# One inference step of a decoder layer on one core: residual pieces fetched ahead, the sample rows' norm in three parts, an earlier token norm, another order of six matmuls

## The chip, the cores and the metric

The kernel runs on one NeuronCore of a Trainium2 chip. The core has five engines with a queue of their own each: TensorE (PE in the profile, with its weight loads as PEld), VectorE (DVE), ScalarE (ACT), GpSimd (POOL) and SyncE (SP), which here issues the DMA transfers. The metric is the device time of one execution in microseconds. For a kernel the median of several runs is given.

## The reference

One layer of a hybrid decoder is computed for 1024 prompt tokens and for 8 samples of 4 new tokens (32 rows), with the same weights. All numbers are 32 bit.

```python
u, v, cq, ckv, kpe = split_in(rms_norm(x, g_mix) @ w_in)
a_out = chunk_gmlp(u, v, w_s, b_s, ln_g, ln_b)              # gated mixing in chunks of 128, width 512
q = mla_queries(rms_norm(cq, g_q_a) @ w_uq)                 # 8 heads, 64 + 32 rope, QK norm
k, vv = mla_keys_values(rms_norm(ckv, g_kv_a), kpe)         # samples: 4096 cached keys beside the new ones
b_out = causal_attention(q, k, vv)                          # width 512
x = x + concat(rms_norm(a_out), rms_norm(b_out)) @ w_o      # output projection, 1024 x 1024
x = x + mem_attend(rms_norm(x, g_mem_x), mk, mv)            # 4 heads x 128, 256 memory tokens
x = x + conv_ffn(rms_norm(x, g_ffn))                        # width 2816, causal convolution of 3
```

The caches, the memory keys and values and the convolution's last rows are results too.

## The kernel before, in words

A 32-bit operand of a matmul is kept as a high and a low part (`split`, lines 200 to 207): ACT casts the source to the high part, DVE subtracts it from the source, which gives the low part. `mm3` (line 185) makes a product from three matmuls per block of the inner dimension: high by high, high by low and low by high.

The stages follow each other: `phase1` (input projection), `phase2a` (attention of the prompt, from about 180 to 400 us), `phase2b` (attention of the samples over the cached pages), `mem_kv` (memory keys and values), `out_proj`, `mem_attention` and the feed-forward part. Inside a block `manual_schedule` the order of the named engines' instructions is the order in which the code issues them. Engines that are not named, and the interleaving of neighbouring blocks, are left to a planner.

**Attention of the prompt.** Units of one head and one half of the queries are cut into steps, 46 in all and a few more. A step transposes probabilities (L1038), computes scores (L1019) of a coming unit, whose maxima DVE takes (L1021, L1025), and multiplies by the values (L1053). Everything else is hung on steps by number with `put(list, steps)`: the splits of the second half's weights, the preparation of keys and queries of a head (`head_prep`, L988 with split L200 to L207), and the projection groups with their norms. `tok_s` is the group of the 32 sample rows for the first four heads: an allocation, two projections, and seven calls that advance a generator, `norm`. Its five parts that do something are: three products on 32 x 4 numbers (L943 to L945); the start of an inverse root (L250 to L252); its first and its second iteration (L259 to L264, four DVE instructions each); and the scaling of the queries with a copy (L954, L955, L959), followed by four POOL instructions for the rotary part (L637 to L640). The rotated queries are wanted when the sample stage starts at step 32.

**Output projection.** The 1056 tokens are three chunks c of 384, 384 and 288 columns (the last 32 are the sample rows), and the 1024 outputs are eight blocks m of 128. `chunk(m, c)` loads the residual piece (L1832, one of four `res` buffers), issues 24 matmuls and returns a function that adds the residual on DVE (L1837), stores the sum (L1838), splits it and squares it on ACT (L1908, L1911). The mixed rows, operands of the matmuls, come from DRAM in eight loads (L1792, three `raw` buffers) and are split in eight calls `split()`: four for chunk 1, then four for chunk 2. `tail[1]`, `tail[2]` and `end()` finish the last sample's attention (L1560 and L1572, then L1333); `mem_out()` issues the six stores of the memory keys and values (L1728, L1730). `mixed_sample` norms the sample rows: square with sum (L1812), inverse root on DVE (L250 to L264), scaling (L1814), then on PE four transposes (L1818), then four splits into chunk 2's operands. SP, PE, ACT and DVE follow the written order in this block.

**Memory attention.** 16 pairs of a head and 256 tokens pass through `scores`, softmax, `trans` (transposition, then a split into `th` and `tl`) and `values`, which multiplies them by the memory values `vh`, `vl` and writes PSUM bank `t`.

Of the kernel before, what the change touches and what calls it, by code (L numbers as in the profile page):

```python
# [5 lines left out]
F32 = mybir.dt.float32  # L6
# [7 lines left out]
P = 128  # L14
# [7 lines left out]
CH = [(0, 384), (384, 384), (768, 288)]  # L22
# [131 lines left out]
class Net:  # L154
# [41 lines left out]
    def split(self, hi, lo, src, g=None, eng="act"):  # L196

        nc, first = self.nc, None
        if g is None:
            first = {"act": nc.scalar.copy, "pool": nc.gpsimd.tensor_copy, "dve": nc.vector.tensor_copy}[eng](hi, src)  # L200
            low = lambda: nc.vector.tensor_tensor(lo, src, hi, ALU.subtract)  # L201
        else:
            if eng == "act":
                first = nc.scalar.activation(hi, src, AF.Copy, scale=g)
            else:
                {"pool": nc.gpsimd, "dve": nc.vector}[eng].tensor_scalar(hi, src, g, None, ALU.mult)
            low = lambda: nc.vector.scalar_tensor_tensor(lo, src, g, hi, ALU.mult, ALU.subtract)  # L207
        if self.lows is None:
            self.low = low()
        else:  # L210
            self.lows.append(low)
        return first
# [463 lines left out]
    def phase2a(self):  # L676
        nc, tc, I, O = self.nc, self.tc, self.I, self.O
        p = self.open("p2q")
# [4 lines left out]
        p = self.open("p2")  # L683
# [19 lines left out]
        c = {"ggq": ggq, "cmask": cmask, "rq": rq, "kss": self.kss, "qt": self.qt}  # L703
# [24 lines left out]
        tok_s, _ = self.proj_group(p, pp, 0, *groups[2], st[0], c)  # L728
# [12 lines left out]
        def put(fs, ts):  # L741
            for f, t in zip(fs, ts):
                extra[t].append(f)
# [5 lines left out]
                jobs[starts[n - 1] + at[e]].append((units[n], e))  # L749

        put(split_w, (7, 8, 13, 15))
        put(tok_s, (4, 4, 5, 17, 18, 19, 20, 21, 21, 21))
        put(preps[1][2:], (3, 4))
        for h in range(2, 8):
            b = 7 * (h - 1)
# [27 lines left out]

        E = mybir.EngineType
        with tc.manual_schedule(engines={E.PE, E.Activation, E.DVE, E.Pool}):
            for f in preps[0][0], preps[0][1], v1[0], norm[0], norm[1]:
# [399 lines left out]
    def phase2b(self):  # L1186
# [22 lines left out]
        def at(n, pos, f, *a):  # L1209
            ev.setdefault((n, pos), []).append(lambda: f(*a))  # L1210
# [38 lines left out]
        for b in range(NB):  # L1249
# [17 lines left out]
            for k, pos, f in ((0, 3, tail[0]), (2, 2, tail[1]), (3 if b == NB - 2 else 4, 3, tail[2])):  # L1267
                if b < NB - 1:
                    at(n + k, pos, f)
        E = mybir.EngineType  # L1270

# [43 lines left out]

        with tc.manual_schedule(engines={E.PE, E.Activation, E.DVE, E.Pool}):
            steps(-10, last + 1)

        with tc.manual_schedule(engines={E.SP, E.PE, E.Activation, E.DVE}):
            self.close("ps3")  # L1320
# [486 lines left out]
    def mixed_sample(self, p, pp, hi, lo):  # L1807

        nc = self.nc
        n = self.t(p, [NS, 512], F32, "n")  # L1810
        r = self.t(p, [NS, 1], F32, "r")
        nc.scalar.activation(n, self.b_s, AF.Square, accum_out=r)  # L1812
        self.rsqrt(p, r, r, 1.0 / 512)
        nc.scalar.activation(n, self.b_s, AF.Copy, scale=r)  # L1814
        yield
        tp = self.t(self.ppt, [P, 512], F32, "o", 1).rearrange("p (k n) -> p k n", k=4)[:, :, :NS]
        for k in range(4):
            nc.tensor.transpose(tp[:, k], n[:, k * P : k * P + P], self.ident[:NS, :NS])  # L1818
        for k in range(4):
            self.split(hi[:, k], lo[:, k], tp[:, k], self.col("g_ab", 4 + k))  # L1820
        yield

    def out_proj(self, pp, p, mxs, load, split, tail, xh, xl, r3, end):
        nc, I = self.nc, self.I
        acc, ws = self.acc, self.ws
        self.pad(acc[2], 2)

        def chunk(m, c):
            o, n = CH[c]
            wh, wl = ws[m]  # L1830
            res = self.t(p, [P, 384], F32, "res", 4)[:, :n]
            nc.sync.dma_start(res, I["xT"][:, 8 * o + m * n : 8 * o + m * n + n])  # L1832
            ps = self.t(pp, [P, 512], F32, "b", 6)[:, :n]
            self.mm3(ps, [(wh[:, k], wl[:, k]) for k in range(8)], [(mxs[c][0][:, k], mxs[c][1][:, k]) for k in range(8)])

            def out():
                nc.vector.tensor_tensor(res, ps, res, ALU.add)  # L1837
                nc.sync.dma_start(self.res_dram[:, m, o : o + n], res)  # L1838
                w = min(NP_ - o, n)
                self.split(xh[:, m, NS + o : NS + o + w], xl[:, m, NS + o : NS + o + w], res[:, :w])  # L1840
                if c == 2:
                    self.split(xh[:, m, :NS], xl[:, m, :NS], res[:, w:])
                self.square(self.pm, acc[c][:, :n], res, m)

            return out

        sample = self.mixed_sample(p, pp, *(x[:, 4:, 256:] for x in mxs[2]))
        E = mybir.EngineType
        with self.tc.manual_schedule(engines={E.SP, E.PE, E.Activation, E.DVE}):
            for _ in range(3):  # L1850
                load()
            split()
            load()
            x = chunk(0, 0)
            split()
            load()
            tail[1]()
            split()
            load()
            self.mem_out()  # L1860
            x()
            split()
            load()
            x = chunk(1, 0)
            tail[2]()
            x()
            split()
            load()
            x = chunk(2, 0)
            end()  # L1870
            split()
            w3 = self.t(self.wr, [P, 8, P], F32, "raw")
            nc.sync.dma_start(w3, I["w_o"][3])
            x()
            x = chunk(0, 1)
            split()
            split()
            next(sample)
            x()
            x = chunk(1, 1)  # L1880
            next(sample)
            x()
            chunk(2, 1)()
            chunk(0, 2)()
            ws[3] = self.stream(None, 8, raw=w3)
            chunk(1, 2)()
            chunk(2, 2)()
        for m in range(3, 10):
            if m > 4:
                chunk(m - 2, 2)()  # L1890
            if m < 7:
                ws[m + 1] = self.stream(I["w_o"][m + 1], 8)
            if m < 8:
                chunk(m, 0)()
                chunk(m, 1)()
        for c in range(2):
            self.token_roots(p, self.t(self.ppt, [P, 512], F32, "om"[c], 1), r3, c)
# [17 lines left out]
    def mem_attention(self, xh, xl, r3):  # L1915
        nc, tc, I, O = self.nc, self.tc, self.I, self.O
# [7 lines left out]
        ps_, p = self.open("pas"), self.open("pa")  # L1924
# [3 lines left out]
        vh, vl = (self.t(p, [P, 2, 512], FR, n) for n in ("vh", "vl"))  # L1928
# [20 lines left out]
        first = (0, 2, 5, 7)  # L1949
# [57 lines left out]
        def values(i):  # L2007
            h, g = units[i][0], order[units[i][1]]
            th, tl = ts.pop(i)
            t, hd = slice(g * 256, g * 256 + 256), slice(h * P, h * P + P)  # L2010
            ps = bank("t", 2)[:, :256]
            self.mm3(ps, [(vh[:, k, hd], vl[:, k, hd]) for k in range(2)], [(th[:, k], tl[:, k]) for k in range(2)])
            self.split(qh[:, h, t], ql[:, h, t], ps)


        sample = {}
# [76 lines left out]
        def slot(s):  # L2093
            c, h = divmod(s, 4)
            if s >= 5:
                scores(s - 5)
            if c > 1 and h == 0:
                roots(c - 1)
            query(h, c)
            if c == 1 and h == 0:  # L2100
                roots(0)
            if s >= 7:
                values(s - 7)
            if h == 3:
                square_sums(c)
            if s >= 6:
                trans(s - 6)
# [5 lines left out]
        with tc.manual_schedule(engines={E.PE}):  # L2113
# [26 lines left out]
            r = self.t(self.pw, [P, 10], F32, "hr")  # L2140
# [38 lines left out]
            for s in range(16, 23):  # L2179
                if s < 21:  # L2180
                    scores(s - 5)
                if s == 16:
                    roots(3)
                if s in VALUES:
                    sample_values(2 * VALUES.index(s))
                if s == 21:
                    sample_out()
                if s > 18:
                    ahead(*divmod(s - 19, 2))
                values(s - 7)  # L2190
                if s < 22:
                    trans(s - 6)
# [57 lines left out]
        for j in (1, 2, 3, 0):  # L2250
# [3 lines left out]
            if j == 2:  # L2254
                sums(0, q[:, 0])
                first = self.weights(0, NK, sums=0)
# [453 lines left out]
```

## Time and profile before

| what | value |
|---|---|
| median of 3 runs | 1813.22 us (1810.88 to 1813.76) |
| the profiled execution | 1813.55 us, its span 1811.8 us |
| mean granted clock of TensorE | 0.997 |
| PE busy | 1787.5 us, 99% of the span |
| DVE, ACT, POOL busy | 1349.3, 920.3, 697.4 us |
| moved by DMA | 261.05 MB, mean 144 GB/s |

A line of the profile names the line of the kernel, the engine, the operation, and result and operands as out<-in. "[2.67 <-DMA res<-xT]" behind an instruction says that its engine sat idle for 2.67 us before it and that the landing of the transfer `res<-xT` ended this. Lines of waits read: who waited, for whom, total in us, number of times, longest. Rows of stretches give, from a start to an end in us, the length, then for PE, PEld, DVE, ACT and POOL the busy time and the number of instructions, then TensorE's granted clock as a share of full speed, the share of DMA time and GB/s. Matmuls are pipelined, and their durations overlap in the timeline; the distance of two starts is what one costs.

### The profile page before, as it was taken

What the parts mean: (1) busy time and instruction counts of PE and PEld (TensorE: products, weight loads), DVE (VectorE), ACT (ScalarE), POOL (GpSimd) and SP (SyncE); (2) the same over time, 40 slices, a digit from 0 to 9 for tenths busy, and PEclk for the clock granted to TensorE, in tenths of its full rate; (3) what the DMA queues carried; (4) which work ended last, traced back from release to release, by engine and by line L of the source; (5) the groups of instructions that cost most, each with busy time, mean ns of one, the idle gap of its engine ahead of it and who ended that gap; (6) DMA issues with size and microseconds to landing.
All of it is one profiled execution on the core that took longest, in us unless ns stands there. A gap on an engine that the chain in (4) does not pass through costs nothing.

```text
span 1811.8 us, 39356 instructions
## 1 busy us (share of the span) xinstructions
PE 1787.5 (99%) x14254; PEld 1694.4 (94%) x14254; DVE 1349.3 (74%) x2777; ACT 920.3 (51%) x1930; POOL 697.4 (38%) x844
## 2 busy tenths in 40 slices
PE   9999999999999999999999999999999999999999
PEld 8999776769899999999799989999999999999999
DVE  7864767657688777787744678998888888878664
ACT  7335776766556555566434467433333333344442
POOL 1021656634445445552023001476677777400000
PEclk9999999999999999999999999999999999999999
DMA  8101353558776666664655245122222222585242
GB/s 324 48 18 62 118 188 117 181 167 227 213 212 179 197 190 190 173 193 127 185 167 189 103 161 184 63 92 86 72 71 81 73 78 88 154 314 165 88 147 78
DMA packets 153043, 261.05 MB, mean 144 GB/s; under 512 B 20881, under 2 KB 97394, under 8 KB 152850
## 3 DMA queue, kind: packets, MB, share of 16 engines
q1 hardware_dynamic: 152850, 258.55, 45.8%
q8 instruction: 112, 1.84, 0.4%
q14 instruction: 81, 0.66, 0.1%
HBM read 212.66 MB, written 45.82 MB: 143 GB/s over the span
## 4 chain that ended last, share of the span: by engine, by line
PE 75%; DVE 5%; ACT 3%; DMA 2%; issue 2%; SPq 1%; POOL 0%; DVEq 0%; ACTq 0%; POOLq 0%
PE s L185 19%; PE d L185 12%; PE E L185 7%; PE F L185 7%; PE X L185 7%; PE b L185 7%; PE A L185 3%; PE s L1019 2%; PE o L1053 2%; PE o L1548 2%; PE tp L1038 1%; PE tp L185 1%; DMA cT<-cT 1%; PE s L1426 1%; PE tp L988 1%
## 5 line engine op out<-in xcount | busy, mean ns | idle before, releaser
L185 PE MATMUL s<-w2h,ch 128*128 128x256 f32 x1018 | 302.6, 297 | 0.0
L185 PE MATMUL s<-w2h,cl 128*128 128x256 f32 x1018 | 294.4, 289 | 2.0 <-DVE cl L1411 2.0
L185 PE MATMUL s<-w2l,ch 128*128 128x256 f32 x1018 | 293.7, 289 | 0.0
L185 PEld LDWEIGHTS s<-w2h,ch 128*128 128x128 f32 x1018 | 192.3, 189 | 3.2 <-issue 2.9
L185 PEld LDWEIGHTS s<-w2h,cl 128*128 128x128 f32 x1018 | 192.1, 189 | 2.6 <-DVE cl L1411 2.2
L185 PEld LDWEIGHTS s<-w2l,ch 128*128 128x128 f32 x1018 | 192.5, 189 | 0.0
L1462 DVE TENSOR_REDUCE ss<-sq 128x16 f32<-128x1024 f32 x128 | 155.2, 1213 | 29.4 <-ACT sq L1459 29.3
L1411 POOL TENSOR_TENSOR cl<-cT,ch 128x512 fp32r<-128x512 f32 x64 | 86.2, 1346 | 195.3 <-ACT ch L1407 189.4
L1459 ACT ACTIVATE sq<-s 128x512 f32<-128x512 f32 x128 | 76.4, 597 | 72.9 <-PE s L185 72.7
L200 ACT CAST a<-brb 128x528 fp32r<-128x528 f32 x77 | 48.8, 634 | 109.4 <-PE d L185 108.2
L1456 ACT ACTIVATE sq<-s 128x512 f32<-128x512 f32 x128 | 76.6, 598 | 49.5 <-PE s L185 39.3
L201 DVE TENSOR_TENSOR a<-brb,a 128x528 fp32r<-128x528 f32 x77 | 54.1, 706 | 55.3 <-ACT a L200 55.1
L185 PE MATMUL d<-a,w 128*128 128x264 f32 x768 | 95.2, 285 | 0.0
L185 PEld LDWEIGHTS d<-a,w 128*128 128x128 f32 x768 | 94.2, 189 | 0.0
L2342 POOL TENSOR_TENSOR lo<-s,hi 128x1024 fp32r<-128x1024 f32 x20 | 63.8, 3190 | 45.7 <-ACT hi L2341 45.7
L2398 ACT COPY a<-A 128x264 f32<-128x264 f32 x43 | 16.1, 374 | 121.2 <-PE A L185 113.8
L185 PE MATMUL mm<-wlo,xh 128*128 128x256 f32 (+3 forms) x272 | 77.1, 286 | 0.1
L185 PE MATMUL mm<-whi,xh 128*128 128x256 f32 (+3 forms) x272 | 77.1, 285 | 0.0
L185 PE MATMUL mm<-whi,xl 128*128 128x256 f32 (+3 forms) x272 | 76.9, 287 | 0.0
L1407 ACT CAST ch<-cT 128x512 fp32r<-128x512 f32 x128 | 73.6, 628 | 0.2 <-issue 0.2
L2464 POOL TENSOR_TENSOR cv<-cv,row 128x1056 f32<-128x1056 f32 x22 | 65.1, 2960 | 20.4 <-ACT cv L2463 20.4
L185 PE MATMUL d<-a,hi 128*128 128x264 f32 x552 | 72.0, 285 | 0.0
(828 smaller groups left out, 6356.8 us busy)
## 6 DMA issues: line engine op xcount, KB each, us to landing
cT<-cT SPq DMA_DIRECT2D x256, 160.0 KB, 2.7
ck<-ck SPq DMA_DIRECT2D x256, 144.0 KB, 3.6
raw<-w_up SPq DMA_DIRECT2D x44, 512.0 KB, 3.6
wsumd<-wsum SPq DMA_DIRECT2D x26, 512.0 KB, 3.8
actd<-cv SPq DMA_DIRECT2D x44, 264.0 KB, 2.4
brb<-actd SPq DMA_DIRECT2D x44, 264.0 KB, 5.6
wsum<-w_down SPq DMA_DIRECT2D x22, 512.0 KB, 3.7
raw<-wsumd SPq DMA_DIRECT2D x20, 512.0 KB, 3.7
```

The costliest lines, as they stand in the source:

```text
L185: x = self.nc.tensor.matmul(out, l, r, start=first and i == 0, stop=last and i == len(seq) - 1)
L200: first = {"act": nc.scalar.copy, "pool": nc.gpsimd.tensor_copy, "dve": nc.vector.tensor_copy}[eng](hi, src)
L201: low = lambda: nc.vector.tensor_tensor(lo, src, hi, ALU.subtract)
L1019: nc.tensor.matmul(sv, a[:, tq], b[:, kc], start=i == 0, stop=i == 2)
L1053: nc.tensor.matmul(u["o"][g : g + 64, o : o + m * P], s["v"][:, j, h % 4], th[:, z * P : (z + m) * P], start=j == 0, stop=b == len(banks) - 1,
L1407: nc.scalar.copy(d["h"][:, k], src[k])
L1411: (nc.vector if k else nc.gpsimd).tensor_tensor(d["l"][:, k], src[k], d["h"][:, k], ALU.subtract)
L1456: nc.scalar.activation(sq[:, 0], ps[:, :, n0 : n0 + 256], AF.Square)
L1459: nc.scalar.activation(sq[:, 1], pt.rearrange("p (e d) -> p e d", e=2), AF.Square)
L1462: yield lambda: nc.vector.tensor_reduce(s["ss"][:, g0 : g0 + 2].rearrange("p e (z h) -> p z e h", z=2), sq.rearrange("p z e (h d) -> p z e ...
L2342: eng.tensor_tensor(lo, src, hi, ALU.subtract)
L2464: nc.gpsimd.tensor_tensor(cv, cv, row, ALU.mult)
```

## The change

- Sample rows of the first four heads: the five parts of `norm` move from steps 17, 18, 19, 20 and 21 to steps 10, 10, 12, 13 and 13.
- `mixed_sample` stops once more, between the inverse root and the scaling. In the output projection its three parts now stand before the sixth split, between the sixth and the seventh split, and before the eighth.
- Residual pieces: the first four are fetched behind the third load of mixed rows, each further one behind the residual step that frees a buffer; chunks past the ninth fetch for themselves as before.
- The first residual step and the matmuls of chunk (1, 0) stand ahead of `mem_out()` and the fourth split; the load of the fourth block's weights (`w3`) stands behind the seventh split instead of the sixth; the eighth split stands behind the sample's transposes.
- `values` in the memory attention: both blocks' two products with the high part `th` first, then the two with `tl`. The six matmuls are the same.

```diff
-        put(tok_s, (4, 4, 5, 17, 18, 19, 20, 21, 21, 21))
+        put(tok_s, (4, 4, 5, 10, 10, 12, 13, 13, 13, 13))
@@ mixed_sample
         self.rsqrt(p, r, r, 1.0 / 512)
+        yield
         nc.scalar.activation(n, self.b_s, AF.Copy, scale=r)
@@ out_proj
+        ready = []
+
+        def fetch(m, c):
+            o, n = CH[c]
+            res = self.t(p, [P, 384], F32, "res", 4)[:, :n]
+            nc.sync.dma_start(res, I["xT"][:, 8 * o + m * n : 8 * o + m * n + n])
+            ready.append(res)
+
         def chunk(m, c):
...
-            res = self.t(p, [P, 384], F32, "res", 4)[:, :n]
-            nc.sync.dma_start(res, I["xT"][:, 8 * o + m * n : 8 * o + m * n + n])
+            if not ready:
+                fetch(m, c)
+            res = ready.pop(0)
...
+        first = [(m, c) for c in range(3) for m in range(3)]
...
             for _ in range(3):
                 load()
+            for x in first[:4]:
+                fetch(*x)
             split()
             load()
             x = chunk(0, 0)
...
             split()
             load()
+            x()
+            x = chunk(1, 0)
             self.mem_out()
-            x()
             split()
             load()
-            x = chunk(1, 0)
             tail[2]()
             x()
+            fetch(*first[4])
+            x = chunk(2, 0)
+            end()
             split()
             load()
-            x = chunk(2, 0)
-            end()
+            x()
+            fetch(*first[5])
+            next(sample)
+            x = chunk(0, 1)
+            split()
+            next(sample)
             split()
             w3 = self.t(self.wr, [P, 8, P], F32, "raw")
             nc.sync.dma_start(w3, I["w_o"][3])
             x()
-            x = chunk(0, 1)
-            split()
-            split()
-            next(sample)
-            x()
+            fetch(*first[6])
             x = chunk(1, 1)
             next(sample)
+            split()
             x()
-            chunk(2, 1)()
+            fetch(*first[7])
+            x = chunk(2, 1)
+            x()
+            fetch(*first[8])
             chunk(0, 2)()
@@ values in mem_attention
-            self.mm3(ps, [(vh[:, k, hd], vl[:, k, hd]) for k in range(2)], [(th[:, k], tl[:, k]) for k in range(2)])
+            pairs = [(v[:, k, hd], th[:, k]) for k in range(2) for v in (vh, vl)] + [(vh[:, k, hd], tl[:, k]) for k in range(2)]
+            for n, (l, r) in enumerate(pairs):
+                nc.tensor.matmul(ps, l, r, start=n == 0, stop=n == 5)
```

## The prediction

> **What bounds the kernel now.** I read four views in this order: the busy times of the page, TensorE's (PE's) waits over the whole span, the timelines around the longest ones, and stretches of the timeline with their granted clock. First the page:
>
> ```profile
> PE 1787.5 (99%) x14254; PEld 1694.4 (94%) x14254; DVE 1349.3 (74%) x2777; ACT 920.3 (51%) x1930; POOL 697.4 (38%) x844
> ```
>
> PE is busy 1787.5 of 1811.8 us, so everything that a reordering can win lies in the remaining 24 us and in matmuls that run at a lower clock. The waits of PE, longest in total first:
>
> ```profile
> PE o L1818 <- ACT n L1814: 4.1, 1, 4.1
> PE tp L1038 <- ACT pr L1030: 3.0, 5, 1.1
> PE s L185 <- DVE cl L1411: 2.0, 1, 2.0
> PE s L1019 <- DVE pr L1025: 1.9, 5, 1.3
> PE tp L1066 <- DVE rsum L1061: 1.8, 2, 1.5
> PE st L361 <- DVE warm L356: 1.6, 1, 1.6
> PE tp L1038 <- DVE qTl L207: 1.5, 2, 1.3
> PE t L185 <- DVE tl L201: 1.4, 3, 0.7
> ```
>
> The columns are total, number, longest. The change touches the first (transposes of the sample rows in the output projection), the last (memory attention), and, as shown below, the longest single wait of the fourth, fifth and seventh. Around the first wait, stretches give PE, PEld, DVE, ACT and POOL busy time, then the granted clock:
>
> ```profile
> 898.52:902.72 4.20, 4.20 (x25) 4.04 (x24) 1.70 (x3) 1.95 (x5) 0.87 (x1) 1.00 0.83 263
> 902.72:907.02 4.30, 0.16 (x1) 0.00 (x0) 3.63 (x16) 1.88 (x6) 0.15 (x1) 0.74 0.66 205
> 907.02:907.58 0.56, 0.56 (x4) 0.50 (x4) 0.17 (x1) 0.56 (x2) 0.00 (x0) 0.50 0.94 386
> 907.58:911.58 4.00, 4.00 (x13) 4.00 (x13) 2.31 (x7) 2.20 (x7) 0.00 (x0) 0.50 0.38 130
> 911.58:913.72 2.14, 2.14 (x13) 2.14 (x13) 0.16 (x1) 0.00 (x0) 1.01 (x1) 0.98 0.55 167
> ```
>
> The stall is 4.30 us long and then goes on costing: the transposes and the first half of the next chunk run at a granted clock of 0.50. That half takes 4.00 us, the second half of the same chunk 2.14.
>
> **Output projection: why the rows are late, and what the change does.** SyncE's (SP's) queue, DVE and ACT before the stall, and the PE group that makes the sample's rows:
>
> ```profile
> 896.67 0.37 SPq L1792 DMA_DIRECT2D raw<-mix  x1
> 897.10 0.46 SPq L1832 DMA_DIRECT2D res<-xT  x1
> ...
> 901.14 0.42 SPq L1832 DMA_DIRECT2D res<-xT  x1
> ```
> ```profile
> 892.33 1.97 PE L1333 MATMUL m<-wuv,olT 128*32 128x64 f32 x32
> ```
> ```profile
> 900.17 0.56 DVE L1837 TENSOR_TENSOR res<-b,res 128x384 f32<-128x384 f32 x1 [2.67 <-DMA res<-xT]
> ...
> 904.26 0.13 DVE L250 TENSOR_SCALAR rqx<-r 32x1 f32<-32x1 f32 x1
> ...
> 906.05 0.15 DVE L264 SCALAR_TENSOR_TENSOR r<-rqh,rqy 32x1 f32<-32x1 f32 x1
> ```
> ```profile
> 901.61 1.69 ACT L204 ACTIVATE mx2h<-raw,cols 128x256 fp32r<-128x256 f32 x4
> 903.21 0.57 ACT L1812 ACTIVATE n<-m 32x512 f32<-32x512 f32 x1
> ...
> 906.29 0.68 ACT L1814 ACTIVATE n<-m,r 32x512 f32<-32x512 f32 x1 [2.42 <-DVE r L264]
> ```
>
> The rows are there at 894.3, yet ACT squares them at 903.21. Ahead of it on ACT stand the residual step of chunk (2, 0) and two splits, and that residual step waited for its piece: fetched at 897.10, behind a load of mixed rows in SP's order, and added at 900.17. The change fetches four pieces before the fourth mixed load, so the residual steps of chunks (1, 0) and (2, 0) wait only for their matmuls, the latter for those that end near 892.3 where the row above begins. Then I place the work in the new order. DVE adds at 892.4 (0.56), ACT casts and squares (0.9, an estimate from the 0.42 us per ACT operation above and the larger width) and then squares the rows from 894.4 to 895.1. The root on DVE takes 906.20 - 904.26 = 1.94, to 897.1. One split of the mixed rows lies beside it on ACT and behind it on DVE. The scaling takes 0.68, to 897.8. PE wants the rows at 902.7, the end of chunk (1, 1): slack 4.9 us, and no wait. **Won: 4.30 for the wait, 4.00 - 2.14 = 1.86 for the slow half chunk, 0.28 for half of the transposes' 0.56: 6.4.**
>
> Costs at nothing: the four early fetches (0.46 each, 1.8 in all) stand on SP where the next load waits for a split anyway; if that cover failed, four mixed loads and the six stores of memory keys and values behind them would slip by 1.8, less than the slack. The matmuls, DMAs and ACT and DVE instructions are the same in number. What is late next is the last split, now behind the sample's four: it would end near 906.8 (two ACT operations at 0.42 and two DVE ones, behind four steps of ACT and DVE in turn from 903.1 on, 0.6 each by estimate), and chunk (0, 2) starts at 902.7 + 0.3 + 4.2 = 907.2. That is 0.4 us of room, and the split's rows are needed only in the chunk's last quarter; I take no wait, upper bound 1.
>
> **Token norm from steps 17-21 to steps 10-13.** The two places, as stretches:
>
> ```profile
> 240.00:262.40 22.40, 22.25 (x156) 18.17 (x156) 13.65 (x44) 16.55 (x41) 12.08 (x17) 1.00 0.61 195
> 279.00:298.00 19.00, 15.00 (x101) 10.81 (x100) 17.38 (x60) 10.47 (x30) 13.41 (x22) 1.00 0.13 42
> ```
>
> Where it leaves, DVE is busy 17.38 of 19.00 us and PE idle 4.00: three waits on DVE, the longest ones of the list (1.3, 1.5, 1.3). Where it goes, DVE is idle 8.75 of 22.40. The moved DVE instructions there now, some of them:
>
> ```profile
> 280.62 0.46 DVE L261 TENSOR_TENSOR rqa<-rqy 32x8 f32<-32x8 f32 x1
> ...
> 281.66 0.38 DVE L264 SCALAR_TENSOR_TENSOR rqy<-rqh,rqy 32x8 f32<-32x8 f32 x1
> ...
> 285.52 0.14 DVE L259 SCALAR_TENSOR_TENSOR rqa<-rqy 32x8 f32<-32x8 f32 x1
> ...
> 288.98 0.55 DVE L955 TENSOR_TENSOR qs<-qs,hr 32x384 f32<-32x384 f32 x1
> ```
>
> The third part is four instructions from 280.62 to 281.97, 1.35 us, ahead of the score reduction that PE awaits first: that wait of 1.3 goes. The fourth part (four of the 0.14 kind with gaps, 0.64) and the fifth (L955 with two small ones, 0.72) lie before the second wait: DVE is then 1.35 + 0.64 + 0.72 = 2.7 earlier, PE 1.3, and the wait of 1.5 shrinks by 1.4. The third wait follows the same two engines and stays. Won 2.7; the bounds are 0 (the queue stays late for other reasons) and 3.3 (with the stretching of the neighbours by the moved POOL instructions). Inserted: two parts at step 10, one at 12, two at 13, some 4 us of DVE against 8.75 idle; the largest block, 1.4 at step 13, meets idle gaps that leave about 0.8 of it ahead of the next query split. Between 0 and 0.8 I take 0.4, since PE fills that stretch to 22.25 of 22.40 and seldom waits for that split at once. Its four POOL instructions go between weight sums that feed nothing nearby. **Net 2.3.**
>
> A row speaks against this: L261 takes 0.46 where its like L259 takes 0.14, and POOL is busy in 13.41 of those 19 us; at the new place it is busy 12.08 of 22.40. Eighteen instructions stretched by 0.3 would add 5.4 us, within the idle 8.75 only if spread well. [...]
>
> **Low turned weights last.** The memory attention's value product used the low half second; now it comes fifth and sixth. At the longest of these waits:
>
> ```profile
> 1069.12 0.39 PE L185 MATMUL t<-tl,vh 128*128 128x256 f32 x1 [0.74 <-DVE tl L201]
> 1069.35 0.28 PE L185 MATMUL t<-th,vl 128*128 128x256 f32 x1
> ```
>
> Three more matmuls run before the wait, at a pitch of 0.12, so each of the waits gets 0.35 shorter: at most 3 x 0.35 = 1.05, and 0.35 more where only the weight load waited. Where DVE itself sets the pace, an earlier PE only waits longer; bounds 0.3 and 1.4. **I take 1.0.**
>
> **Sum.** The profiled execution took 1813.55 (span 1811.8 and 1.75 around it), 0.33 above the median 1813.22. 1813.55 - 6.4 - 2.3 - 1.0 = **1803.9**.
>
> **Rivals.**
> 1. *The token norm only moves its stall.* For it: DVE's queue at 279-298 is also fed by two other norms. Against: it is the DVE work just ahead of the waits. Then 1813.55 - 6.4 - 1.0 = 1806.1.
> 2. *The wait in the output projection shrinks but stays,* because ACT reaches the rows late behind splits. Here a second place in the trace matters:
>
> ```profile
> 498.50:501.90 3.40, 3.32 (x15) 3.32 (x16) 3.37 (x7) 2.35 (x6) 1.03 (x1) 0.52 0.82 217
> ```
>
> It follows the wait of 2.0 at L185 in the list: the granted clock is 0.52 for 3.4 us. A remaining wait of 2 us would thus keep the slow half chunk; only 2.3 is won there: 1813.55 - 2.3 - 2.3 - 1.0 = 1808.0. [...]
> 3. *Slower: the early fetches hold SP.* The first fetch stands between the fourth and the fifth mixed load in the old order too, but pieces two to four have rooms that no row shows free before their old fetches; the last of those rows is 901.14. SP is in order, so the fourth mixed load would go out only then, land 3.1 later (897.10 to 900.17), be split in 1.4, and chunk (0, 1), due at 894.3, would wait until 905.6: 11.3, and 1.9 of slow clock. 1813.55 - 9.7 + 13.2 = 1817.0. It begins to cost when SP is held past 889.8, and turns the sign past about 897.6. Against it: those rooms were memory of the phase before, as the first piece's was.
> 4. *The change doesn't do what it says:* the queues come out in much the old order, because instructions of two neighbouring blocks are interleaved by a planner. 1813.
>
> **How the numbers follow.** The forecast 0.62, rival one 0.17, two 0.09, three 0.05, four 0.07. Its own range is 1801.5 to 1806.5 (token norm 0 to 3.3, values 0.3 to 1.4). Below that lies the case that the wait at 498 meets the clock differently (1.6); above it rivals one and two, with the runs' scatter of 1.4: 1800.5 to 1809. What can be told from no change here is about 0.2%, 3.6 us: faster means under 1809.6, which the first three cases give: 0.87; same 0.08, slower 0.05.
>
> **What would show it.** Right: no PE wait on the scaled rows, clock 1.00 from 898 to 915, residual additions in which no DMA ended the wait; PE idle under 2 us in the old 279-298; waits on tl under 0.4. Wrong: SP held between the third and the fourth mixed load, a PE wait for mixed rows at chunk (0, 1) or (0, 2), a new PE wait on query splits near 257.

## The result

The changed kernel takes **1801.51 us** (median of 6 runs, 1799.68 to 1804.31), against 1813.49 for the kernel before beside it (6 runs, 1810.48 to 1815.46): a ratio of 0.9938, 95% interval 0.9925 to 0.995. The prediction was 1803.9 with a range of 1800.5 to 1809.0. The profiled execution took 1802.43 us (span 1800.7, mean granted clock 1.000), 11.1 less than the profiled one of before. The number of matmuls and of VectorE instructions is the same; PE's busy time fell by 4.5 us to 1783.0: before ran for 10.2 us at half clock (498.64 to 502.05 and 904.82 to 911.65), where the same matmuls last longer (13 of one chunk 4.00 us there, 13 more of the same chunk 2.14 behind it, at 0.98).

The list of PE's waits of the kernel after (total, number, longest) no longer has the scaled sample rows at its head, and has a new entry, on a load of mv; the lines that bear on the change are:

```profile
PE s L185 <- DVE cl L1411: 1.3, 1, 1.3
PE sx L2097 <- DMA skT<-mv: 1.2, 2, 0.7
PE s L1019 <- DVE pr L1025: 1.1, 5, 0.5
...
PE tp L1038 <- DVE qTl L207: 0.5, 2, 0.3
PE tp L1066 <- DVE rsum L1061: 0.3, 1, 0.3
PE t L2034 <- DVE tl L201: 0.3, 1, 0.3
```

**Output projection.** Stretches of the kernel after around the samples' transposes (length, then PE, PEld, DVE, ACT, POOL, then the granted clock):

```profile
898.00:915.00 17.00, 17.00 (x117) 16.71 (x117) 10.26 (x20) 9.28 (x22) 3.29 (x4) 1.00 0.65 191
898.40:899.00 0.60, 0.60 (x7) 0.33 (x5) 0.00 (x0) 0.00 (x0) 0.00 (x0) 1.00 1.02 398
899.00:903.20 4.20, 4.20 (x25) 4.20 (x25) 2.35 (x7) 2.13 (x7) 0.00 (x0) 1.00 0.17 64
```

PE has no gap there and the clock stays at 1.00. The queues of SP, ACT and DVE of the kernel after show why:

```profile
873.93 2.30 SPq L1834 DMA_DIRECT2D res<-xT  x4
888.25 0.56 DVE L1847 TENSOR_TENSOR res<-b,res 128x384 f32<-128x384 f32 x1 [0.77 <-PE b L185]
892.91 0.68 ACT L1815 ACTIVATE n<-m,r 32x512 f32<-32x512 f32 x1 [1.23 <-DVE r L264]
901.63 0.88 DVE L207 SCALAR_TENSOR_TENSOR mx2l<-raw,cols,mx2h 128x256 fp32r<-128x256 f32 x2
```

The four fetches go out 14 us ahead of the addition at 888.25, which now waits for its matmuls and not for its piece (all 16 waits of the residual additions end with PE). The rows are scaled by 893.6, some 5 us before PE transposes them at 898.4. The last split ends at 902.5, 0.7 ahead of the chunk that reads it.

**Token norm.** The place that the parts left (old 279 to 298) and the place where they went:

```profile
279.00:298.00 19.00, 18.24 (x129) 13.71 (x126) 15.88 (x58) 12.14 (x33) 14.33 (x20) 1.00 0.17 56
240.00:262.40 22.40, 22.25 (x155) 18.17 (x154) 18.16 (x61) 16.56 (x41) 14.66 (x22) 1.00 0.63 203
```

PE is idle for 0.76 instead of 4.00 us in the first, and exactly as busy as before, 22.25 of 22.40, in the second, although DVE went from 13.65 to 18.16 there.

**Where the 11.1 us went.** First and last starts of four lines of PE, before and after:

```profile
L988 PE MATMUL tp<-ident,k x64: 270/273/315, 196.7 to 367.7; 128*96 128x128 f32 x64
L1053 PE MATMUL o<-pth,v x352: 272/379/432, 208.0 to 396.9; 128*64 128x256 f32 x111, 128*64 128x128 f32 x65
L1333 PE MATMUL m<-wuv,olT x32: 219/219/243, 892.3 to 894.1; 128*32 128x64 f32 x32
L2075 PE MATMUL sx<-skT,wxh x64: 272/273/298, 1059.4 to 1071.7; 128*32 128x128 f32 x64
```
```profile
L988 PE MATMUL tp<-ident,k x64: 270/273/315, 196.3 to 364.0; 128*96 128x128 f32 x64
L1053 PE MATMUL o<-pth,v x352: 272/379/431, 207.7 to 393.1; 128*64 128x256 f32 x111, 128*64 128x128 f32 x65
L1333 PE MATMUL m<-wuv,olT x32: 218/219/243, 888.1 to 889.9; 128*32 128x64 f32 x32
L2097 PE MATMUL sx<-skT,wxh x64: 272/273/298, 1048.5 to 1060.5; 128*32 128x128 f32 x64
```

From these rows I cut the span in three. **Segment A** runs from the first L988 to the last L1053 (attention of the prompt), **segment B** from there to the last L1333 (attention of the samples), **segment C** from there to the last samples' value product (output projection and memory attention). Before: 200.2, 497.2, 177.6. After: 196.8, 496.8, 170.6. So A gave 3.4, B 0.4, C 7.0, and 0.4 was there at the start already; 0.1 is lost behind C. In C, 6.3 had been won when the next chunk ended (913.72 before, 903.20 after, less the 4.2 from A, B and the start); 0.7 is the memory attention.

### The profile page after: what moved, and what is told of

Read it like the earlier page. It is cut to its first block, busy times and chain, and to the rows that moved or that the text cites. A ratio compares the mean times of both kernels' runs of the same rounds, so it can differ in the third digit from the quotient of the medians.

```text
span 1800.7 us, 39354 instructions
## 1 busy us (share of the span) xinstructions
PE 1783.0 (99%) x14254; PEld 1690.6 (94%) x14254; DVE 1349.5 (75%) x2777; ACT 919.7 (51%) x1930; POOL 698.5 (39%) x844
## 4 chain that ended last, share of the span: by engine, by line
PE 78%; DVE 3%; ACT 3%; DMA 2%; issue 1%; SPq 1%; POOL 0%; DVEq 0%; POOLq 0%; ACTq 0%
PE s L185 19%; PE d L185 12%; PE b L185 8%; PE E L185 7%; PE F L185 7%; PE X L185 7%; PE A L185 3%; PE s L1019 2%; PE o L1053 2%; PE o L1548 2%; PE tp L1038 1%; PE tp L185 1%; PE s L1426 1%; PE tp L988 1%; PE b L1621 1%
```

## The experiments

The same three segments were read from every run's trace. The ratio is to the kernel before measured beside it, with its 95% interval; two runs have a single execution, the profiled one.

| run | time, us | ratio to before | A | B | C |
|---|---|---|---|---|---|
| before (profile) | 1813.55 | | 200.2 | 497.2 | 177.6 |
| after (profile) | 1802.43 | | 196.8 | 496.8 | 170.6 |
| after, again | 1802.47 | 0.9949 (0.9936 to 0.9963) | 196.7 | 493.7 | 169.6 |
| token norm alone | 1809.38 | 0.9981 (0.9972 to 0.999) | 197.3 | 493.7 | 177.2 |
| output projection alone | 1807.80 | 0.9967 (0.9954 to 0.998) | 202.8 | 496.0 | 171.0 |
| order of the values alone | 1814.26 | 1.0001 (0.9991 to 1.001) | 204.0 | 494.1 | 175.4 |
| four early fetches alone | 1806.98 | 0.9968 (0.9955 to 0.998) | 202.5 | 494.0 | 171.3 |
| after, no early fetch | 1802.11 | 0.9942 (0.9925 to 0.9959) | 197.1 | 494.0 | 171.3 |
| after, fifth part late | 1803.98 | 0.9956 (0.9939 to 0.9972) | 199.6 | 493.7 | 170.6 |
| after, rows late by 11 copies | 1808.28 | one execution | 197.5 | 496.2 | 174.1 |
| after, rows late by 13 copies | 1807.92 | one execution | 196.8 | 493.9 | 177.6 |
| after, samples' values later | 1801.96 | 0.9938 (0.9925 to 0.9952) | 198.0 | 494.3 | other order |
| after, mixed loads earlier | 1801.07 | 0.9934 (0.992 to 0.9947) | 196.8 | 494.0 | 170.2 |
| after, both of these | 1801.57 | 0.9939 (0.9925 to 0.9952) | 199.2 | 493.7 | other order |

The columns show more than the times: A is 196.7 to 199.6 wherever the token norm is (mostly) at its new steps and 200.2 to 204.0 where it isn't; C is 169.6 to 171.3 wherever PE doesn't wait for the sample rows. B holds none of the changed lines, and yet is 2 to 3.5 us longer in four of the executions, the two profiles that I compared among them (see the last section).

### The parts one by one

```diff
 # token norm alone, on the kernel before
-        put(tok_s, (4, 4, 5, 17, 18, 19, 20, 21, 21, 21))
+        put(tok_s, (4, 4, 5, 10, 10, 12, 13, 13, 13, 13))
```

> The kernel before with the token norm's list of steps alone changed to 10, 10, 12, 13, 13, 13, 13. My theory: what TensorE waited for at steps 18 to 21 was work queued on VectorE behind the token norm's parts, so all three waits there (1.25, 1.50 and 1.25 us in the profile of before) shrink together, the idle time of TensorE in the stretch 279 to 298 us falls from 4.0 to about 0.8 us, the inserted parts cost TensorE nothing at steps 10 to 13, and the whole time falls by 3.3 us (2.8 to 3.8). Rival, the prediction's own step: the third wait stays, and the gain is 2.3 us. Rival, the stall only moves: TensorE idles about 4 us longer at steps 10 to 13 and the time falls by less than 0.5 us.

The time fell by 3.4 us by its ratio (1.8 to 5.1), A by 2.9. PE's waits from 279 to 302 in this run:

```profile
PE s L1019 <- DVE pr L1025: 1.0, 1, 1.0
PE tp L1038 <- DVE qTl L207: 0.3, 1, 0.3
```

The second wait of before (1.5, on rsum) is not in the list, the third is 0.3. The rival "the stall only moves" falls, and so does the prediction's step that the third wait stays. But the first wait, which the prediction let go altogether, is still 1.0.

```diff
 # output projection alone: mixed_sample, fetch, chunk and the written order as in the change;
 # token steps and values as before
```

> The kernel before with the output projection's part of the change alone (nine fetches ahead, the new order of splits, the samples' norm in three parts). My theory: the wait of 4.30 us at the samples' transposes and the half clock of the 4.56 us behind it go together, 6.3 us (5.9 to 6.7) off the whole time, with TensorE at clock 1.00 through that place. Rival: a wait of 2 us or more stays there with some microseconds at half clock, and the gain is 4.2 us or less.

The time fell by 6.0 us (3.6 to 8.3), C by 6.6, and no wait on the rows is left. Both agree with 6.3. A is 2.6 longer than in the profile of before, with code there that is the same; that is taken up below.

```diff
 # order of the values alone, on the kernel before
-            self.mm3(ps, [(vh[:, k, hd], vl[:, k, hd]) for k in range(2)], [(th[:, k], tl[:, k]) for k in range(2)])
+            pairs = [(v[:, k, hd], th[:, k]) for k in range(2) for v in (vh, vl)] + [(vh[:, k, hd], tl[:, k]) for k in range(2)]
+            for n, (l, r) in enumerate(pairs):
+                nc.tensor.matmul(ps, l, r, start=n == 0, stop=n == 5)
```

> The kernel before with the order of the six products of the memory attention's values alone changed (the low turned weights last). My theory: the three waits on the low halves, 1.4 us together, fall to about 0.3 us; TensorE then reaches the samples' values earlier against the last loads of mv and waits for these where it did not, up to 1.2 us; the whole time falls by 0.2 to 1.0 us. Rival: without the other two parts the loads of mv land in time, no new wait appears, and the time falls by 1.0 to 1.4 us. Rival: the order changes nothing, under 0.2 us.

The whole time did not move (1.0001, from 1.6 less to 1.8 more), which is too coarse for what was expected. The waits of this run show both halves of the theory:

```profile
PE sx L2077 <- DMA skT<-mv: 0.5, 1, 0.5
PE t L2014 <- DVE tl L201: 0.3, 1, 0.3
```

The waits on the low halves went from 1.4 to 0.3, and a wait of 0.5 on a load of mv stands where none was in the profile of before. C is 2.2 shorter than in before, but some 1.7 of this (half of 3.4) is the clock and not the order: behind the wait on the sample rows this execution ran 3.4 us at half clock (909.0 to 912.4), the profile of before 6.8. In the changed kernel the wait on mv was 1.2 in one execution and 0.3 in another, and C 170.6 and 169.6. The new order is not its only cause: with the old order it is 0 in before and with the four early fetches alone, but 0.2 with the output projection alone and 0.5 with the token norm alone. The last three of these loads are issued right behind four of the weight sums and took 7.3 us to land in the profile of after, 6.2 in that of before. In the profile of the kernel after, SP's queue and the landing (KB each, median us):

```profile
1050.74 1.95 SPq L2058 DMA_DIRECT2D skT<-mv  x3
```
```profile
skT<-mv SPq DMA_DIRECT2D x3, 512.0 KB, 7.3
```

So the order takes 1.1 us of waits away, and 0.3 to 1.2 stands on the loads of mv instead, of which up to 0.5 stands there without the order too. Whether it is worth anything in the whole time the runs do not show.

### Which half of the output projection's change does it

```diff
 # four early fetches alone, on the kernel before
+        # fetch(), and chunk() that takes a fetched piece, as in the change
...
             for _ in range(3):
                 load()
+            for x in ((0, 0), (1, 0), (2, 0), (0, 1)):
+                fetch(*x)
             split()
```

> The kernel before with four pieces of the residual fetched ahead and nothing else: old order of splits and chunks, the samples' norm in two parts, later pieces fetched in their chunk. Theory A: the wait at the samples' transposes came from the residual additions ending late on VectorE, because their pieces landed late; with the pieces ahead the scaled rows are ready near 899.7 us, before TensorE gets there at 902.7, and the gain is all of the output projection's, 6.3 us (5.8 to 6.7). Theory B: the order of the norm's parts between the splits is needed as well; the wait stays at 2 us or more, its half clock too, and the gain is 0 to 3 us.

The time fell by 5.8 us (3.6 to 8.2 by the interval of the ratio), C by 6.3. The samples' rows in this run (durations, first and last start):

```profile
L1818 PE MATMUL o<-ident,n x4: 221/222/243, 902.4 to 902.6; 32*128 32x32 f32 x4
...
L1814 ACT ACTIVATE n<-m,r x1: 683/683/683, 898.1 to 898.1; 32x512 f32<-32x512 f32 x1
```

Scaled at 898.8, 3.6 us ahead of the transposes. Theory A holds: the order of the norm's parts was not needed.

```diff
 # the changed kernel without early fetches (the new order stays)
-            for x in first[:4]:
-                fetch(*x)
...
-            fetch(*first[4])
...
-            fetch(*first[8])
```

> The changed kernel without any fetch ahead: each residual piece is fetched in its chunk again, and the new order of splits and the norm's three parts stay. The run with four fetches ahead alone gave all of the output projection's gain. Theory A: either half of this part is enough by itself, since the norm's scaling now stands ahead of two splits; the samples' rows are ready near 895 us, TensorE gets there at about 898.5, no wait appears, and the time is the changed kernel's within 1 us (about 1801.5). Theory B: only the fetches do it; without them VectorE again waits for the pieces, the rows come late, TensorE waits 2 us or more with some microseconds at half clock, and the time is 3 to 6 us above the changed kernel's.

1802.11, the changed kernel's time. Theory A holds again. The residual addition does wait for its piece, and nothing follows from it:

```profile
888.93 0.56 DVE L1847 TENSOR_TENSOR res<-b,res 128x384 f32<-128x384 f32 x1 [1.91 <-DMA res<-xT]
```
```profile
L1815 ACT ACTIVATE n<-m,r x1: 678/678/678, 893.1 to 893.1; 32x512 f32<-32x512 f32 x1
```

The rows are scaled at 893.8, and PE transposes them at 897.0. **Either half of this part is enough; together they win what one wins.** The fetches alone leave 3.6 us of slack, the order alone 3.2, both together some 5.

### Which part of the token norm makes which wait

```diff
 # the changed kernel with the fifth part (scaling on VectorE, rotary part on GpSimd) back at step 21
-        put(tok_s, (4, 4, 5, 10, 10, 12, 13, 13, 13, 13))
+        put(tok_s, (4, 4, 5, 10, 10, 12, 13, 21, 21, 21))
```

> The changed kernel with the token norm's last three parts (the scaling on VectorE and the rope on GpSimd) back at step 21, the four parts before them at the new steps. Theory A: the waits at old 283 and 294 us are due to the parts of steps 17 to 20 and stay away; the wait at old 297 us (1.25 us in before, 0.29 in after) comes back to about 0.7 to 1.3 us, and phase 2a ends 0.5 to 1.0 us later than in the changed kernel. Theory B: the third wait shrank only because the schedule ahead of it had moved; it stays at 0.3 us and nothing changes.

PE's waits from 278 to 302 in this run:

```profile
PE tp L1066 <- DVE rsum L1061: 1.5, 1, 1.5
PE tp L1038 <- DVE qTl L207: 1.3, 1, 1.3
PE s L1019 <- DVE pr L1025: 0.2, 1, 0.2
```

Neither theory foresaw this: **both** later waits are back, at the size that they had before (1.5 and 1.3), and the first is gone. A is 2.8 longer than in the kernel after. One part of 0.72 us on DVE brings 2.8 us of waits. This is not the scatter of one execution: the wait on rsum is 1.5 and the one on the query split 1.0 to 1.3 in all four executions with the old steps, while the nine others with the new steps have no wait on rsum there and 0.3 to 0.7 on the split. How, its DVE and GpSimd queues show:

```profile
288.05 0.55 DVE L955 TENSOR_TENSOR qs<-qs,hr 32x384 f32<-32x384 f32 x1
...
290.36 0.77 DVE L262 TENSOR_TENSOR rqa<-rqa,rqx 128x32 f32<-128x32 f32 x1
291.17 0.65 DVE L263 SCALAR_TENSOR_TENSOR rqh<-rqa 128x32 f32<-128x32 f32 x1
```
```profile
288.74 0.45 POOL L637 TENSOR_TENSOR rp<-qs,tq_c 32x128 f32<-32x128 f32 x1 [7.72 <-DVE qs L955]
...
290.36 0.73 POOL L637 TENSOR_TENSOR rp<-q,tq_c 128x256 f32<-128x256 f32 x1
```

GpSimd waits 7.72 us for the sample queries, with the rotary part of the next head queued behind them. Both then run beside the next norm's small instructions on DVE, which take up to 0.77. In the repeated run of the changed kernel GpSimd had done that head's rotary part by 286.4, and the same instruction with nothing beside it is

```profile
289.34 0.19 DVE L262 TENSOR_TENSOR rqa<-rqa,rqx 128x32 f32<-128x32 f32 x1
```

The eight instructions of the root (L259 to L264) last from 288.60 to 292.05 in the one and from 288.22 to 289.98 in the other: 3.45 against 1.76. In the profile of before they last from 289.53 to 292.98, the same 3.45. So 0.7 us of DVE's delay is the part itself, and 1.7 (3.45 - 1.76) goes with what runs beside the root on GpSimd: the part's own rotary half and the one that it held up.

### How long a gap of TensorE costs its clock

```diff
 # the changed kernel, with the samples' rows made late (13 in the second run)
         nc.scalar.activation(n, self.b_s, AF.Copy, scale=r)
+        for _ in range(11):
+            nc.gpsimd.tensor_copy(n, n)
         yield
```

> The changed kernel with eleven copies of the samples' scaled rows onto themselves on GpSimd between scaling and transposes, so that the rows come some 6 us later (0.55 us each, estimated from the copy of twice the size at line 1102 that takes 1.03 us): a wait of about 1.2 us at the transposes. Theory of the rows (waits of 1.25, 1.33 and 1.50 us left the clock at 1.00, waits of 1.66 and 1.96 us brought 3.4 us at half): the clock stays at 1.00 and the loss is the wait alone. Rival: any wait lowers the clock, and about 1.7 us more are lost.

> The same with thirteen copies: a wait of about 2.3 us at the transposes. Theory of the rows: half clock for about 3.4 us from 1 to 2 us after the gap's end or its last part, so 1.7 us lost beside the wait, about 4 us in all. [...]

The copies took 0.60 us and followed each other at 0.71, so the gaps came out longer than meant: 2.72 and 4.07 us. Stretches of the run with eleven:

```profile
899.58:902.30 2.72, 0.01 (x2) 0.01 (x1) 0.00 (x0) 0.00 (x0) 2.41 (x4) 1.00 0.58 220
902.30:903.45 1.15, 1.15 (x8) 1.11 (x9) 0.25 (x1) 0.37 (x2) 0.00 (x0) 1.00 0.00 0
903.45:906.85 3.40, 3.40 (x12) 3.40 (x12) 2.10 (x6) 1.74 (x6) 0.00 (x0) 0.51 0.00 0
```

and with thirteen:

```profile
896.23:900.30 4.07, 0.00 (x1) 0.00 (x0) 0.00 (x0) 0.00 (x0) 3.65 (x7) 0.97 0.42 161
900.30:906.70 6.40, 6.40 (x22) 6.33 (x23) 2.92 (x8) 2.88 (x8) 0.78 (x1) 0.50 0.19 30
```

After 2.72 us of idling the clock holds for another 1.15 us and is then halved for 3.40; after 4.07 us it is halved at once for about twice that. C is 3.5 and 7.0 longer than in the kernel after, near the gap and the slow time together (2.72 + 1.7, 4.07 + 3.2, less what the waits on mv give back: these were 0.4 and 1.1 here, 1.2 in after). Both gaps are longer than the waits of 1.66 and 1.96 us that the theory of the rows took from other runs, and half clock followed as it did there; but over all runs it is not a matter of length alone (see the last section).

### Two tries at a better version

```diff
 # samples' values later
-        SCORES, VALUES = (8, 9, 10, 11), (16, 17, 18, 19)
+        SCORES, VALUES = (8, 9, 10, 11), (16, 17, 19, 20)
 # mixed loads earlier
-                at(8 * k + 24, 0, mixed_load, k)
+                at(8 * k + 23, 0, mixed_load, k)
```

> The changed kernel unaltered, as the yardstick of its neighbours on the same chip: 1801.5 us (1800 to 1804), with waits of about 1.2 us on the loads of mv at the samples' values.

> The changed kernel with the samples' values of the memory attention at slots 16, 17, 19 and 20 instead of 16 to 19, so that the fifth to eighth load of mv has a slot more to land. Theory: the waits of TensorE on the loads of mv (1.2 us in two in after) are what gave back half of the reordered values' gain; they go, no other appears, and the time is 1.2 us (0.8 to 1.5) under the changed kernel's. Rival: the copy and the transposes of the samples' output, now straight behind their values, make a wait of 1 us or more, and nothing is won.

> The changed kernel with each load of the mixed latents issued a step earlier (8k+23 for 8k+24). The wait on the low half of the chunk near 494 us was 2.0 us in before, 1.3 in after, 0.8 and 0 in others: it is a matter of when a load lands. Theory: it goes in every execution, and with it the half clock that the longest of them bring; 0.5 to 1.3 us under the changed kernel. Rival: the earlier load meets other traffic and nothing changes.

> The changed kernel with both of these edits. If they act in different places they add: 1.3 to 2.8 us under the changed kernel, about 1799.5 us.

None is to be told from the changed kernel: 1802.47 beside 1801.96, 1801.07 and 1801.57, with intervals that overlap. With the samples' values later the waits on mv are gone, but PE now waits for turned weights instead (waits of this run):

```profile
PE t L2034 <- ACT th L200: 0.9, 1, 0.9
...
PE t L2034 <- DVE tl L201: 0.7, 2, 0.5
```

In after these were 0.3 in all. The rival's outcome holds, in another place than it was put: the turned weights come late, not the samples' output. With the mixed loads earlier the wait near 494 is absent, but it was absent in the repeated run of the changed kernel too, so that execution shows nothing for the edit.

## Why the prediction was right, and where its steps were off

The forecast's likeliest case came about, and every rival fell: no PE wait is left on the rows, the clock is 1.00 from 898 to 915, no residual addition waits for a DMA, PE's idle time in the old 279 to 298 is 0.76, the waits on tl are 0.3. The terms, by the two profiles:

| step | predicted | profiles | alone, whole time |
|---|---|---|---|
| output projection | 6.4 | 6.3 | 6.0 (3.6 to 8.3) |
| token norm, net | 2.3 | 3.4 | 3.4 (1.8 to 5.1) |
| low turned weights last | 1.0 | 0.7 | -0.2 (-1.8 to 1.6) |
| sample stage and start, no edit there | 0 | 0.8 | |
| behind C | 0 | -0.1 | |
| sum | 9.7 | 11.1 | |

By the two times that the whole change was measured it is worth 11.2 us (9.1 to 13.6) and 9.2 (6.7 to 11.6); the parts alone add up to 9.2. The forecast of 9.7 agrees with both, but partly by luck, as the terms show: 0.8 of the 11.1 between the two profiles lies where nothing was edited, and two errors of the token norm's term go against each other. The prediction's own range is also added up wrongly: with its terms it runs from 1813.55 - 6.4 - 3.3 - 1.4 = 1802.5 to 1813.55 - 6.4 - 0 - 0.3 = 1806.9, not from 1801.5 to 1806.5, so that the median of 1801.5 lies 1 us below it and within the wider range only. (The three chances for faster add up to 0.88, not 0.87.)

- **Output projection.** The term was right to 0.1, and "what is late next" was too: the last split has 0.7 us of room for a forecast 0.4. Rival three (SP held by the early fetches) fell: they took 2.30 us on SP at 873.93, the rooms were free. Where the working implied that both edits were needed, it was too careful: each wins all of it by itself.
- **Token norm: the term mis-sized was "won 2.7".** The step "the third wait follows the same two engines and stays" failed: it fell from 1.25 to 0.29. The late fifth part shows why. The prediction counted its 0.72 on DVE and named the stretching by its GpSimd instructions only for the upper bound of 3.3; the queues put 1.7 us on that stretching (it was not tested apart from the 0.72), and both later waits hang on the fifth part. Three of the four executions with the old steps also ran 3.4 or 6.8 us at half clock behind the first wait (1.66 to 2.67 us long there); the profile of before, where it is 1.25, did not, so that a prediction from this one trace could not count them. "That wait of 1.3 goes" failed as well, the other way: 0.5 of it stayed, 1.0 in the run with the token norm alone. "Inserted 0.4" was 0: PE's busy time at the new steps is 22.25 of 22.40 as before. The stretch of 0.3 for each instruction, which the prediction took from one row (0.46 against 0.14), was no upper limit: with the values alone two instructions of 0.15 last 0.96 and 0.97 (last section).
- **Values.** The waits on tl fell by 1.1, as taken (1.0), but the prediction looked at no transfer behind them. A wait on the loads of mv stands there now: 1.2 in this profile, 0.3 in the next. So the 0.7 by which the memory attention is shorter in the table is not these waits, which cancel; PE's idle time there went from 1.75 to 1.61 only, the rest lies in time that counts as busy, and the runs do not say where.
- **The profile of before as the basis.** Its segment B held a wait of 2.0 us at 496 and 3.4 us at half clock, its segment A the shortest wait of its place (below). The two deviations are about 3.5 too long and, by the three other executions with the old token norm (A of 202.5 to 204.0), 2.3 to 3.8 too short. They about cancel in its time, which would be why it stood near the median, and they do not cancel in the terms.

## What to carry to other kernels

Cost a moved instruction by what runs beside it, not by its own duration: here eight DVE instructions took 3.45 us beside a GpSimd half that came late and 1.76 without, where the moved DVE half itself takes 0.7. Where two edits take away the same wait, one of them may do; test each alone before keeping both. And a longer wait of TensorE is worth more than its length: in the fourteen traces all nine gaps of 1.66 us and more were followed by 3.4 or 6.8 us at half clock, of the nineteen from 1.2 to 1.5 us one was.

## What the runs showed of the hardware that was not expected

**Some DVE instructions lasted until a GpSimd instruction ended, and a small shift changed which engine's got longer.** The run with the values alone has the old token norm; the wait that is 1.25 us in the profile of before is 2.67 there. DVE and GpSimd just ahead of it:

```profile
282.05 0.96 DVE L263 SCALAR_TENSOR_TENSOR rqh<-rqa 32x8 f32<-32x8 f32 x1
283.05 0.97 DVE L264 SCALAR_TENSOR_TENSOR rqy<-rqh,rqy 32x8 f32<-32x8 f32 x1
```
```profile
281.96 1.04 POOL L964 TENSOR_TENSOR k<-k,hr 128x512 f32<-128x512 f32 x1
282.96 1.05 POOL L965 TENSOR_TENSOR k<-kr,hr 128x512 f32<-128x512 f32 x1
```

Two instructions that take 0.15 us each with the output projection alone last 0.96 and 0.97 here, and each ends within 0.02 us of the end of the GpSimd instruction that had begun before it. In the profile of before it is the other way round: GpSimd's L964 lasts 1.65 us (from 281.98) for 1.04 here, and DVE's L964, which runs from 282.05 beside it, 0.67. In the run with both tries DVE's L964 lasts 1.60 us where it takes 0.68 in the repeated run of the changed kernel, and again it meets L965 of GpSimd (280.41 to 281.46). PE's first wait was 1.3, 2.0, 2.7 and 1.7 with the old token norm, 0.2 to 1.2 with the new. Together with the half clock that follows the longer ones (by estimate 1.7 us lost for each 3.4 at 0.50) this makes up most of A's scatter from execution to execution.

**In these traces the clock falls in spells of 3.4 us, and the length of a gap does not decide it alone.** Gaps of 1.21, 1.25, 1.33 and 1.50 us left the clock at 1.00. One of 1.24 us, in the run with both tries, did not:

```profile
284.72:288.12 3.40, 3.40 (x15) 2.49 (x12) 2.19 (x8) 1.24 (x2) 1.88 (x4) 0.54 0.00 0
```

Nor did one of 1.66 (four early fetches alone) and one of 1.96 (output projection alone), each with one spell of 3.4 us that began 1.3 and 1.5 us after the gap's end; the second:

```profile
281.45:283.41 1.96, 0.00 (x1) 0.01 (x1) 1.80 (x8) 1.20 (x5) 0.22 (x1) 1.00 0.00 0
284.95:288.35 3.40, 3.40 (x15) 2.27 (x16) 2.25 (x13) 0.08 (x1) 0.00 (x0) 0.50 0.00 0
```

Gaps of 2.67, 4.07 and 4.30 us had two spells on end, that of 2.72 one; but with the values alone a gap of 3.95, and with the token norm alone one of 4.37, had one only. The last of these (896.19 to 900.56), in stretches as long as a spell, the third of which is the spell:

```profile
894.50:897.91 3.41, 1.69 (x10) 1.38 (x8) 2.78 (x6) 2.92 (x8) 1.01 (x1) 1.00 0.53 181
897.91:901.32 3.41, 0.76 (x6) 0.72 (x7) 2.35 (x13) 1.49 (x4) 0.00 (x0) 1.00 0.90 285
901.32:904.74 3.42, 3.42 (x13) 3.42 (x12) 1.74 (x6) 1.38 (x6) 0.00 (x0) 0.50 0.38 137
```

In the first of these PE is busy for 1.69 of 3.41 us and the clock of the next stays at 1.00; in the second it is busy for 0.76, and half clock follows. The 3.41 us up to the half clock behind the gap of 1.24 have at least 2.17 us of busy PE (3.41 - 1.24), and half clock followed all the same. So in these runs neither the length of a gap nor PE's busy share of the 3.4 us before decides it alone; what does was not found.

**The sample stage scatters by one late load.** Segment B is 493.7 to 494.3 in ten of the fourteen executions, and 496.0 to 497.2 in four, each time with a wait of 0.8 to 2.0 us on the low half of a chunk between 494 and 499. That chunk's split on ACT waits there for a load of mixed latents (2.6 to 3.7 us), which is issued late and does not land slowly: in these four SP sends it 95.1 to 96.1 us after the end of segment A, in the eight others with the load at its step 92.6 to 93.5, and it takes 3.3 to 3.8 us in all twelve. What holds SP back ahead of it was not found.
